# Up projection by channels: the weights as left operand, one pool of PSUM banks behind the mixer, the embedding ahead of it

## The chip, the core and the metric

The kernel runs on one core of a Trainium2 chip, as one program. A core has engines that each work through their own instructions in order and wait for each other by semaphores: TensorE (PE in the profile, with its weight loads as PEld), VectorE (DVE), ScalarE (ACT), GpSimd (POOL) and SyncE (SP, which here only issues transfers). TensorE multiplies a left operand, which is loaded ahead as weights (128 contraction rows x 128 columns here), with a right operand that streams through (128 contraction rows x up to 512 columns), and adds the product to a bank of PSUM; a bank holds 128 partitions x 512 float32, and there are eight. The metric is the device time of one execution in microseconds (us). Three executions of the kernel before took 1487.59, 1486.27 and 1486.39 us; the median is 1486.39.

## The reference

One layer of a hybrid decoder over 256 tokens (T) with a model width of 2048 (D), all in float32. Its first part, the mixer (state space heads and windowed attention, then an output projection that is added to h), is the same in both kernels. The rest is this:

```python
u = _rmsnorm(h, ffn_norm_g[i]) @ w_up[i]                  # 2048 -> 2 x 5632 channels
u = _causal_dwconv(u, ffn_conv_w[i], ffn_conv_b[i])       # 3 taps along the tokens, channel by channel
g_ff, u_ff = jnp.split(u, [D_FF], axis=-1)
h = h + (jax.nn.silu(g_ff) * u_ff) @ w_down[i]            # 5632 -> 2048
gate = jax.nn.sigmoid(_rmsnorm(h, ple_norm_g[i]) @ w_ple_gate[i])
pe = _rmsnorm(p[i] @ w_ple_proj[i], ple_post_g[i])        # the embedding: 256 -> 2048
h = h + gate * pe
```

`_rmsnorm` divides a token's row by the root of its mean square and multiplies each channel with a gain. The convolution shifts along the tokens, with weights of its own for each channel.

## The kernel before, in words

**Numbers and products.** Every operand of a matmul is split into a high part (a cast to a shorter type, `S.copy` on ScalarE, L195) and a low part (the rest, a subtraction on VectorE, L196). A product takes three matmuls into the same bank: high times high weights (L231), high times low weights (L232), low times high weights (L233). The left operand is a tile of activations, 128 channels x 128 tokens; the right operand is 128 channels x 512 columns of the weights; so a result has the tokens on its partitions, one bank for each of the two blocks of 128 tokens (`acc_pair`).

**Weights.** `load_w` (L201) loads 512 KB, a tile of 128 x 1024, from SyncE's queue into one of five buffers, ScalarE casts it (L195) and VectorE subtracts (L196), into four buffers each. One such tile serves two contraction steps of 128 of one chunk of 512 columns.

**Left operands.** Activations with tokens on the partitions have to be transposed to become a left operand: `transpose_split` (L257) lets TensorE transpose 128 x 128 pieces (L264) into a bank, and ScalarE and VectorE split the result (with a gain for each channel, L198 and L199) into the high and low tiles of an `Lhs` (L240 and on).

**Stages.** The mixer ends with output projections; the last one (L750) runs after the last attention heads, in four slices of 512 columns. After each slice `add_to_h` (L365) adds it to h, and `next_lhs` (L370) squares the new part of h (L374, for the norm) and transposes it unscaled, with the gains, into `hT`. The norm's factor `rh`, one number for each token, follows from all four slices (`finish_rstd`, L377). Two loads stand on ScalarE's queue here: the convolution's weights `fcw` (L759) and the transposed p (L766), which goes into the space of `pe` and is split into `ph` and `pl`. These tiles lie in space that the mixer's pools held until then.

The up stage (`up`, L784) runs over 22 chunks of 512 channels, eleven for the gate and eleven for u. A chunk takes eight weight tiles and 16 contraction steps of six matmuls, 96 in all. ScalarE moves its two banks out and multiplies with `rh` (L790), since the tokens lie on the partitions there. Then `conv_chunk` (L284) transposes the result, eight times 128 x 128 (L291), into two banks of the pool `ps_tr`, so that the channels lie on the partitions, and `conv_tile` (L275) makes the first tap with the bias on ScalarE (L278) and two more on VectorE (L280). Silu, the product with u (GpSimd) and a split make it the left operand of the down projection, which runs in six segments of up to two pairs of chunks, each one segment late. The last segment's projection squares and transposes h again for the gate. Then `embed` (L769) runs: four slices of two contraction steps, 48 matmuls, copied out to `pe` by VectorE (L778) and squared by ScalarE (L780). Last comes the gate stage: the post gain is loaded (on SyncE's queue), `pe` is normed, and for each of four slices 96 matmuls (L223) are followed by sigmoid, multiplication, addition and the store.

**What sets the order.** The code is recorded first, and a scheduler places it by a model of the engines: each engine's order is fixed when the program is built. Each pool's buffers set how far the work ahead may run: PSUM's eight banks belong to `ps_acc` (two tags, two buffers each), `ps_tr` (two) and `ps_ms` (two, used by the mixer).

## Time and profile before

| | before |
|---|---|
| median of three runs | 1486.39 us |
| the profiled execution | 1487.57 us |
| its span, from first to last instruction | 1485.8 us |
| mean granted TensorE clock | 1.000 |
| 0 to 637.4: mixer and output projections | 637.4 us, PE busy 632.11 |
| 637.4 to 1380.9: up and down projections | 743.5 us, PE busy 743.50 |
| 1380.9 to 1392.7: embedding | 11.8 us, PE busy 11.80 |
| 1392.7 to 1485.8: gate | 93.1 us, PE busy 88.08 |

The stages are stretches that were cut at the first and last matmul of each stage, read from the timeline; busy times are those of the view by windows. "Busy" of TensorE counts the modelled ends of pipelined matmuls, so busy is not the same as at its peak. A row of the timeline gives start and duration of an instruction in us, the engine, the line, the operation, result and operands; x6 at its end means six of them drawn together. A row of a group gives the count, the summed busy time in us, the mean of one in ns, and the idle time of the engine ahead of them. A row of windows gives from:to and length, the busy time of PE, PEld, DVE, ACT and POOL with their counts, then the granted clock, the share of the DMA engines and GB/s. In the strip by slices a 9 means nine tenths or more.

### The profile page before, as it was taken

The page shows a single profiled execution, that of the slowest core. Times are in us where ns is not written, and L with a number is a line of the kernel's source. Part 1 is how long each engine was busy: PE and PEld are TensorE (multiplying, and loading weights), DVE is VectorE, ACT ScalarE, POOL GpSimd, SP SyncE. Part 2 cuts the span into 40 slices and gives each one's busy share as a digit, 9 for nine tenths or more (in the row PEclk, how much of TensorE's full clock was granted, in tenths as well). Part 3 has the DMA queues.
Part 4 walks back from the last instruction along what each step waited for, and adds up shares of the span by engine and source line. Part 5 has one row for each costly group of instructions (what it writes and reads, how often), then busy time and mean ns, then how long its engine had stood idle before and what let it go on. Part 6 is the DMA issues. An engine that isn't in the chain of part 4 may idle for free.

```text
span 1485.8 us, 18615 instructions
## 1 busy us (share of the span) xinstructions
PE 1475.5 (99%) x6884; PEld 1213.0 (82%) x6884; DVE 977.0 (66%) x1290; ACT 800.3 (54%) x1111; POOL 159.2 (11%) x152
## 2 busy tenths in 40 slices
PE   9999999999999999999999999999999999999998
PEld 6887888888787888888888888888888888888887
DVE  7568776656769687766556656565665556566854
ACT  7575555646555454565555445545553554454643
POOL 1004022044033030000000000000000000000000
PEclk9999999999999999999999999999999999999999
DMA  9565665655555545366666666666566666656672
GB/s 338 180 205 170 202 184 167 185 158 179 145 164 148 157 148 163 115 196 199 185 186 187 191 188 184 185 196 187 184 191 191 184 188 192 185 186 189 206 226 100
DMA packets 79099, 271.67 MB, mean 183 GB/s; under 512 B 8752, under 2 KB 11504, under 8 KB 78624
## 3 DMA queue, kind: packets, MB, share of 16 engines
q1 hardware_dynamic: 78176, 269.55, 59.2%
q8 instruction: 54, 0.88, 0.2%
q10 hardware_dynamic: 720, 0.74, 0.1%
q0 software_dynamic: 112, 0.19, 0.1%
q14 instruction: 37, 0.30, 0.1%
HBM read 268.32 MB, written 2.13 MB: 182 GB/s over the span
## 4 chain that ended last, share of the span: by engine, by line
PE 95%; DMA 2%; DVE 1%; POOL 1%; issue 1%; ACT 0%; SPq 0%; DVEq 0%; POOLq 0%
PE acc L233 27%; PE acc L232 27%; PE acc L231 27%; PE acc L223 5%; PE tr L291 2%; PE ms L656 1%; PE acc L329 1%; PE ms L505 1%; PE acc L330 1%; PE acc L331 1%; DMA seg<-scr 1%; PE tr L264 1%; PE tr L688 1%; DMA w<-in_w_in_dram 1%; PE ms L698 0%
## 5 line engine op out<-in xcount | busy, mean ns | idle before, releaser
L196 DVE TENSOR_TENSOR wl<-w,wh 128x1024 fp32r<-128x1024 f32 (+1 forms) x493 | 617.8, 1256 | 396.5 <-ACT wh L195 395.1
L195 ACT CAST wh<-w 128x1024 fp32r<-128x1024 f32 (+1 forms) x493 | 516.5, 1050 | 485.7 <-PE acc L233 380.2
L232 PE MATMUL acc<-wl,ah 128*128 128x512 f32 x1168 | 457.0, 391 | 1.2 <-DVE wl L196 1.1
L233 PE MATMUL acc<-wh,al 128*128 128x512 f32 x1168 | 457.5, 394 | 0.0
L231 PE MATMUL acc<-wh,ah 128*128 128x512 f32 x1168 | 457.3, 393 | 0.0
L232 PEld LDWEIGHTS acc<-wl,ah 128*128 128x128 f32 x1168 | 219.4, 188 | 47.0 <-DVE wl L196 2.1
L231 PEld LDWEIGHTS acc<-wh,ah 128*128 128x128 f32 x1168 | 219.5, 188 | 45.7 <-issue 1.8
L233 PEld LDWEIGHTS acc<-wh,al 128*128 128x128 f32 x1168 | 219.0, 188 | 44.5 <-issue 0.8
L233 PE MATMUL acc<-wh,gl 128*128 128x512 f32 x352 | 137.6, 391 | 0.0
L231 PE MATMUL acc<-wh,gh 128*128 128x512 f32 x352 | 137.4, 390 | 0.0
L232 PE MATMUL acc<-wl,gh 128*128 128x512 f32 x352 | 137.2, 390 | 0.0
L806 POOL TENSOR_TENSOR cv<-cv,cv 128x1024 f32<-128x1024 f32 x11 | 35.5, 3228 | 649.2 <-DVE cv L280 649.2
L231 PE MATMUL acc<-wh,yh 128*128 128x512 f32 x256 | 100.2, 395 | 0.0
L232 PE MATMUL acc<-wl,yh 128*128 128x512 f32 x256 | 100.1, 392 | 0.0
L233 PE MATMUL acc<-wh,yl 128*128 128x512 f32 x256 | 99.8, 394 | 0.0
L280 DVE SCALAR_TENSOR_TENSOR cv<-tr,fcw,cv 128x254 f32<-128x254 f32 (+1 forms) x176 | 74.0, 476 | 19.8 <-ACT cv L278 19.8
L368 DVE TENSOR_TENSOR h<-h,acc 128x512 f32<-128x512 f32 x112 | 73.8, 680 | 6.0 <-PE acc L233 5.7
L232 PEld LDWEIGHTS acc<-wl,gh 128*128 128x128 f32 x352 | 66.1, 188 | 13.6
L233 PEld LDWEIGHTS acc<-wh,gl 128*128 128x128 f32 x352 | 66.1, 188 | 13.5
L231 PEld LDWEIGHTS acc<-wh,gh 128*128 128x128 f32 x352 | 66.1, 188 | 13.4
L278 ACT ACTIVATE cv<-tr,fcw 128x256 f32<-128x256 f32 x88 | 44.8, 559 | 34.3 <-PE tr L291 34.3
L233 PEld LDWEIGHTS acc<-wh,yl 128*128 128x128 f32 x256 | 48.1, 188 | 10.6 <-issue 1.0
(248 smaller groups left out, 1362.6 us busy)
## 6 DMA issues: line engine op xcount, KB each, us to landing
w<-in_w_up_dram SPq DMA_DIRECT2D x176, 512.0 KB, 3.7
w<-in_w_in_dram SPq DMA_DIRECT2D x127, 512.0 KB, 3.8
w<-in_w_down_dram SPq DMA_DIRECT2D x88, 512.0 KB, 3.7
w<-in_w_out_dram SPq DMA_DIRECT2D x64, 512.0 KB, 3.6
w<-in_w_pg_dram SPq DMA_DIRECT2D x32, 512.0 KB, 4.2
seg<-scr SPq DMA_DIRECT2D x8, 512.0 KB, 6.0
h<-in_x_dram SPq DMA_DIRECT2D x2, 1024.0 KB, 8.4
w<-in_w_pe_dram SPq DMA_DIRECT2D x4, 512.0 KB, 4.3
```

Of the source, the lines that this page charges most:

```text
L195: S.copy(hi, src)
L196: V.tensor_tensor(out=lo, in0=src, in1=hi.bitcast(F32), op=ALU.subtract)
L223: PE.matmul(acc[b], lhsT=l, rhs=r, start=(k == 0 and m == 0), stop=(k == total - 1 and m == 2))
L231: PE.matmul(acc[b], lhsT=hi, rhs=wh[:, i, :], start=(k == 0), stop=False)
L232: PE.matmul(acc[b], lhsT=hi, rhs=wl[:, i, :], start=False, stop=False)
L233: PE.matmul(acc[b], lhsT=lo, rhs=wh[:, i, :], start=False, stop=(k == total - 1))
L264: PE.transpose(tr[:, i, b * P : (b + 1) * P], src[b][:, f * P : (f + 1) * P], ident)
L278: S.activation(out=dst, in_=ps, func=AF.Identity, scale=taps[n - 1], bias=bias)
L280: V.scalar_tensor_tensor(out=dst[:, s:], in0=ps[:, : T - s], scalar=taps[n - 1 - s], in1=dst[:, s:], op0=ALU.mult, op1=ALU.add)
L291: PE.transpose(tr[:, i, b * P : (b + 1) * P], src[b][:, f * P : (f + 1) * P], ident)
L368: V.tensor_tensor(out=hs, in0=hs, in1=acc[b], op=ALU.add)
L806: G.tensor_tensor(out=cg, in0=cg, in1=cu, op=ALU.mult)
```

## The change

In `up`, the weights become the left operand, 128 input channels x 128 output channels, and the activations the right one. A chunk has four banks, one for each 128 channels, with the high and the low part of the activations side by side as 512 columns (2 x 256 tokens). For each contraction step and channel tile there are two matmuls: high weights times both halves (512 columns, L824 of the changed kernel) and low weights times the high half (256 columns, added to the second half of the bank, L825). So a chunk has 128 matmuls. ScalarE copies the first half of a bank out, VectorE adds the second, and the sum has the channels on its partitions already: it goes straight to `conv_tile`, with no transposes.

Since tokens now lie along the free axis there, `rh` can't be applied behind the product: h is multiplied with `rh` before it is transposed (L808, on VectorE). So the last output projection only squares its slices, and the 32 transposes of h follow when `rh` is known. `embed` is called ahead of them in place of behind the last down projection. The pools of PSUM of the mixer are closed there, and one pool `ps_b` of four tags with two buffers serves the embedding, the transposes, the up, down and gate stages. `Lhs` keeps high and low in one tile, so that both can be streamed as one operand.

```diff
@@ -92,9 +92,11 @@
     act = ctx.enter_context(tc.tile_pool(name="act", bufs=1))
     const = ctx.enter_context(tc.tile_pool(name="const", bufs=1))
     small = ctx.enter_context(tc.tile_pool(name="small", bufs=2))
-    ps_acc = ctx.enter_context(tc.tile_pool(name="ps_acc", bufs=2, space=PSUM))
-    ps_tr = ctx.enter_context(tc.tile_pool(name="ps_tr", bufs=2, space=PSUM))
-    ps_ms = ctx.enter_context(tc.tile_pool(name="ps_ms", bufs=2, space=PSUM))
+    banks = ExitStack()
+    ps_acc = banks.enter_context(tc.tile_pool(name="ps_acc", bufs=2, space=PSUM))
+    ps_tr = banks.enter_context(tc.tile_pool(name="ps_tr", bufs=2, space=PSUM))
+    ps_ms = banks.enter_context(tc.tile_pool(name="ps_ms", bufs=2, space=PSUM))
+    ps_b = []

     uid = [0]

@@ -117,10 +119,22 @@
         if n:
             G.memset(sb(pool, [P, n // 4], "fill", bufs=1), 0.0)

+    def bank(i):
+        return ps_b[0].tile([P, NC], F32, tag=f"b{i}", name=nm(f"bank{i}"))
+    took = [0, 0]
     def acc_pair():
+        if ps_b:
+            took[0] ^= 2
+            return [bank(took[0] + b) for b in range(NB)]
         return [ps_acc.tile([P, NC], F32, tag=f"acc{b}", name=nm(f"acc{b}")) for b in range(NB)]

     def tr_tile():
+        if ps_b:
+            took[1] = (took[1] + 1) % 4
+            return bank(took[1])
         return ps_tr.tile([P, NC], F32, tag="tr", name=nm("tr"))

     def ms_tile():
@@ -241,14 +255,15 @@


         def __init__(self, pool, kt, tag):
-            self.t = [
-                (sb(pool, [P, KG, T], f"{tag}h{g}", F32R), sb(pool, [P, KG, T], f"{tag}l{g}", F32R))
-                for g in range((kt + KG - 1) // KG)
-            ]
+            self.both = [sb(pool, [P, KG, 2, T], f"{tag}{g}", F32R) for g in range((kt + KG - 1) // KG)]
+            self.t = [(t[:, :, 0, :], t[:, :, 1, :]) for t in self.both]

         def part(self, k):
             h, l = self.t[k // KG]
             return h[:, k % KG, :], l[:, k % KG, :]
+        def pair(self, k):
+            return self.both[k // KG][:, k % KG, :, :]

         def __call__(self, k, b):
             h, l = self.part(k)
@@ -367,11 +382,14 @@
             hs = hres[b][:, n * NC : (n + 1) * NC]
             V.tensor_tensor(out=hs, in0=hs, in1=acc[b], op=ALU.add)

-    def next_lhs(lhs, ss, n, gain):
-
+    def squares(ss, n):
         for b in range(NB):
             sq = sb(small, [P, NC], "hsq")
             S.activation(out=sq, in_=hres[b][:, n * NC : (n + 1) * NC], func=AF.Square, accum_out=ss[:, b, n : n + 1])
+    def next_lhs(lhs, ss, n, gain):
+        squares(ss, n)
         transpose_split([hres[b][:, n * NC : (n + 1) * NC] for b in range(NB)], lhs, 4 * n, gain)

     def finish_rstd(ss, tag):
@@ -603,7 +621,6 @@
                 project(*held.pop(0))


-    hT = Lhs(act, KT, "a")
     ssh = sb(small, [P, NB, 4], "ssh", bufs=1)
     with tc.tile_pool(name="att_s", bufs=2) as as_, tc.tile_pool(name="att", bufs=2, reuse_waits="tile") as ap_:
         qscaled = sb(as_, [P, HD], "qgs", bufs=1)
@@ -747,10 +764,12 @@
                 project(*held.pop(0))
             prev_ = done
         fill(as_)
-        project(*prev_, lambda n: next_lhs(hT, ssh, n, g_ffn))
+        project(*prev_, lambda n: squares(ssh, n))

     rh = finish_rstd(ssh, "rh")
     mix.close()
+    banks.close()
+    ps_b.append(ctx.enter_context(tc.tile_pool(name="ps_b", bufs=2, space=PSUM)))


     pp = ctx.enter_context(tc.tile_pool(name="pe", bufs=1))
@@ -781,16 +800,36 @@

     with tc.tile_pool(name="ffn", bufs=2) as fp:

+        embed()
+        hT = Lhs(act, KT, "a")
+        for n in range(4):
+            hs = [sb(fp, [P, NC], f"hs{b}") for b in range(NB)]
+            for b in range(NB):
+                V.tensor_scalar_mul(hs[b], hres[b][:, n * NC : (n + 1) * NC], rh[:, b : b + 1])
+            transpose_split(hs, hT, 4 * n, g_ffn)
         def up(c):
-            acc = acc_pair()
-            gemm(acc, hT, [w_up[c, g] for g in range(KT // KW)])
-            t = []
-            for b in range(NB):
-                u_ = sb(fp, [P, NC], f"u{b}")
-                S.activation(out=u_, in_=acc[b], func=AF.Copy, scale=rh[:, b : b + 1])
-                t.append(u_)
+            acc = [bank(f) for f in range(4)]
+            for s in range(KT // KW):
+                wh, wl = load_w(w_up[c, s])
+                for i in range(KW):
+                    k = s * KW + i
+                    hl = hT.pair(k)
+                    for f in range(4):
+                        fs = slice(f * P, (f + 1) * P)
+                        PE.matmul(acc[f], lhsT=wh[:, i, fs], rhs=hl, start=(k == 0), stop=False)
+                        PE.matmul(acc[f][:, T:], lhsT=wl[:, i, fs], rhs=hl[:, 0, :], start=False, stop=(k == KT - 1))
             cv = sb(fp, [P, 4, T], f"cv{c // NPAIR}")
-            conv_chunk(t, cv, fcw, 3, 4 * c)
+            for f in range(4):
+                w = fcw[:, (4 * c + f) * 4 : (4 * c + f + 1) * 4]
+                u_ = sb(fp, [P, T], f"u{f}")
+                S.copy(u_, acc[f][:, :T])
+                V.tensor_tensor(out=u_, in0=u_, in1=acc[f][:, T:], op=ALU.add)
+                conv_tile(u_, cv[:, f, :], [w[:, j : j + 1] for j in range(3)], w[:, 3:4])
             return cv

         pair = 0
@@ -811,7 +850,6 @@
             pair += np_
         h2T = Lhs(act, KT, "a")
         project(*pending.pop(), lambda n: next_lhs(h2T, ssg, n, g_ple))
-        embed()
     rg = finish_rstd(ssg, "rg")
```

TensorE at the border between two chunks of the up stage, before: `acc` are the banks of the next chunk, `tr` those of the transposes, `u` the chunk that has just been moved out, `ah` and `al` the high and low part of the transposed h, `wh` and `wl` those of the weights.

```order
L231 MATMUL acc_1430_6921<-wh_6941,ah_507_2628 128x512
L232 MATMUL acc_1430_6921<-wl_6942,ah_507_2628 128x512
L291 MATMUL tr_6895<-ident_114,u_1424_6890 128x128
L291 MATMUL tr_6906<-ident_114,u_1424_6890 128x128
L233 MATMUL acc_1430_6921<-wh_6941,al_508_2629 128x512
L231 MATMUL acc_1429_6920<-wh_6941,ah_507_2628 128x512
L232 MATMUL acc_1429_6920<-wl_6942,ah_507_2628 128x512
L233 MATMUL acc_1429_6920<-wh_6941,al_508_2629 128x512
L291 MATMUL tr_6895<-ident_114,u_1425_6892 128x128
L291 MATMUL tr_6895<-ident_114,u_1424_6890 128x128
```

The same border in the changed kernel: `bank` is a bank of the new pool, `a` the tile with both parts of the transposed h.

```order
L824 MATMUL bank_1259_5976<-a_1237_5882,wh_6133 128x512
L825 MATMUL bank_1259_5976<-a_1237_5882,wl_6134 128x256
L824 MATMUL bank_1260_5977<-a_1237_5882,wh_6133 128x512
L825 MATMUL bank_1260_5977<-a_1237_5882,wl_6134 128x256
L824 MATMUL bank_1290_6180<-a_1234_5879,wh_6185 128x512
L825 MATMUL bank_1290_6180<-a_1234_5879,wl_6186 128x256
L824 MATMUL bank_1291_6181<-a_1234_5879,wh_6185 128x512
L825 MATMUL bank_1291_6181<-a_1234_5879,wl_6186 128x256
```

The transposes are gone, and long and short matmuls alternate, each with another tile of weights.

TensorE between the last output projection and the up stage, before: the projection's last slice has transposes of h (`h_1`, `h_2`, the two token blocks) among its matmuls, and the next rows are those of the first up chunk.

```order
L231 MATMUL acc_1240_5867<-wh_5869,ah_507_2628 128x512
L232 MATMUL acc_1240_5867<-wl_5870,ah_507_2628 128x512
L264 MATMUL tr_5692<-ident_114,h_1_84 128x128
L264 MATMUL tr_5692<-ident_114,h_2_85 128x128
L264 MATMUL tr_5692<-ident_114,h_1_84 128x128
L264 MATMUL tr_5692<-ident_114,h_2_85 128x128
L233 MATMUL acc_1239_5866<-wh_5869,al_508_2629 128x512
L233 MATMUL acc_1240_5867<-wh_5869,al_508_2629 128x512
L231 MATMUL acc_1239_5866<-wh_5887,ah_507_2628 128x512
```

The changed kernel there: the projection's last matmuls (`y` is its left operand) and the first of the embedding (`ph` is the high part of p).

```order
L245 MATMUL acc_1187_5699<-wh_5719,y_1044_5049 128x512
L246 MATMUL acc_1187_5699<-wl_5720,y_1044_5049 128x512
L247 MATMUL acc_1187_5699<-wh_5719,y_1044_5049 128x512
L245 MATMUL bank_1206_5775<-wh_5778,ph_5766 128x512
L246 MATMUL bank_1206_5775<-wl_5779,ph_5766 128x512
L245 MATMUL bank_1207_5776<-wh_5778,ph_5766 128x512
```

Of the 48 embedding matmuls 16 that need only `ph` come first, four for each slice; then each slice's other eight; then the 32 transposes of the scaled h (`hs`), and behind the last of these the up stage:

```order
L279 MATMUL bank_1252_5953<-ident_114,hs_1251_5950 128x128
L279 MATMUL bank_1253_5962<-ident_114,hs_1251_5950 128x128
L279 MATMUL bank_1253_5962<-ident_114,hs_1250_5949 128x128
L279 MATMUL bank_1253_5962<-ident_114,hs_1251_5950 128x128
L824 MATMUL bank_1259_5976<-a_1234_5879,wh_5979 128x512
L825 MATMUL bank_1259_5976<-a_1234_5879,wl_5980 128x256
L824 MATMUL bank_1260_5977<-a_1234_5879,wh_5979 128x512
```

Up matmuls, which stood among the transposes of h, now stand behind all of them.

VectorE in this place of the changed kernel: the copies of the embedding's banks into `pe` (L797), low halves of weights (L210), the scaling of the third and fourth slice of h (L808) and the first low halves of the transposed h (L213).

```order
L797 COPY pe_1199_5760<-bank_1227_5853 128x512
L210 TENSOR_TENSOR wl_6024<-w_6022,wh_6023 128x1024
L797 COPY pe_1200_5761<-bank_1228_5854 128x512
L808 TENSOR_SCALAR hs_1246_5927<-h_1_84,rh_5748 128x512
L808 TENSOR_SCALAR hs_1250_5949<-h_1_84,rh_5748 128x512
L808 TENSOR_SCALAR hs_1247_5928<-h_2_85,rh_5748 128x512
L210 TENSOR_TENSOR wl_6046<-w_6044,wh_6045 128x1024
L808 TENSOR_SCALAR hs_1251_5950<-h_2_85,rh_5748 128x512
L213 SCALAR_TENSOR_TENSOR a_1234_5879<-bank_1241_5896,gains_92,a_1234_5879 128x256
```

The first four scalings stand ahead of the first copy of the embedding, these four behind the last, since `hs` has two buffers a block.

ScalarE's queue at the border, in the changed kernel: the squares of h (L388), the two loads, casts of weights (L209), the cast of p (`ph`) and the squares of the embedding (L799).

```order
L388 ACTIVATE hsq_5738,ssh_2620<-h_1_84 128x512 [waits DVE_49,Activation_49]
L778 DMA fcw_5762<-in_ffn_cw_dram 128x352 [waits PE_49]
L785 DMA pe_1199_5760<-in_pT_dram 128x512
L209 CAST wh_5856<-w_5855 128x1024 [waits DMAHW1_49]
L388 ACTIVATE hsq_5740,ssh_2620<-h_2_85 128x512 [waits DVE_49,Activation_49]
L209 CAST ph_5766<-pe_1199_5760 128x512 [waits DMAHW6_49]
L799 ACTIVATE hsq_5796,ssp_5768<-pe_1199_5760 128x512 [waits DVE_49,Activation_49]
L209 CAST wh_5979<-w_5978 128x1024 [waits DMAHW2_49,PE_49]
```

Before, the load of `fcw` stood one square earlier and that of p at the same place; high halves of h and casts of up weights stood where the squares of the embedding stand now.

## The prediction

> **What bounds the kernel.** I read the page first: span, engine shares, granted clock, chain of waits. Times are microseconds; this profiled execution took 1487.57, of which 1485.8 are its span, and the median of the runs shown is 1486.39. I work out a difference against this execution and add it to the median, since both are the same kernel 0.1% apart.
>
> ```profile
> span 1485.8 us, 18615 instructions
> PE 1475.5 (99%) x6884; PEld 1213.0 (82%) x6884; DVE 977.0 (66%) x1290; ACT 800.3 (54%) x1111; POOL 159.2 (11%) x152
> PEclk9999999999999999999999999999999999999999
> PE 95%; DMA 2%; DVE 1%; POOL 1%; issue 1%; ACT 0%; SPq 0%; DVEq 0%; POOLq 0%
> ```
>
> TensorE has hardly a gap and carries 95% of the chain. So every matmul slot saved is time saved and every TensorE gap added is time lost, one for one; work on VectorE (66%) or ScalarE (54%) counts only where TensorE comes to wait for it. Durations of matmuls overlap, so I never add them up: I take the distance from one start to the next, from the timeline.
>
> **Removed: the transposes of the up result.** Here is one chunk boundary of the up stage.
>
> ```profile
> L291 PE MATMUL tr<-ident,u 128*128 128x128 f32 x176 | 26.3, 272 | 0.0
> 904.74 0.39 PE L233 MATMUL acc<-wh,al 128*128 128x512 f32 x1
> ...
> 913.36 0.40 PE L232 MATMUL acc<-wl,ah 128*128 128x512 f32 x1
> ...
> 914.74 0.82 PE L291 MATMUL tr<-ident,u 128*128 128x128 f32 x6
> ...
> 921.11 0.39 PE L232 MATMUL acc<-wl,ah 128*128 128x512 f32 x1
> ```
>
> From 904.74 to 913.36 stand 38 steps of 512-wide matmuls: 8.62 / 38 = 0.2268 each. From 913.36 to 921.11 stand 30 such steps and the eight transposes of one chunk (two before the six that are shown): 7.75 - 30 x 0.2268 = 0.95 for eight, 0.119 each with the disturbance behind them. Twenty-two chunks (176 in the group's row) make **-20.9**, all on the bound engine. The 32 transposes of h ahead of the up stage stay; they only move.
>
> **Added: short matmuls.** Per contraction step a chunk had six 512-wide matmuls; now it has, for each of four channel tiles, one 512-wide (high weights times high and low activations side by side) and one 256-wide (low weights times high). The columns are the same, 4 x 768 = 6 x 512, but there are 22 x 16 x 4 = 1408 pairs of a long and a short one in place of 1.5 long ones, 0.3402 each. A steady alternation of the two widths occurs nowhere in this trace; the nearest is in the attention, where they are mixed.
>
> ```profile
> 408.54 0.28 PE L696 MATMUL ms<-ph,vh 128*128 128x256 f32 x1
> 408.66 0.28 PE L697 MATMUL ms<-ph,vl 128*128 128x256 f32 x1
> 408.77 0.40 PE L231 MATMUL acc<-wh,ah 128*128 128x512 f32 x1
> 409.01 0.40 PE L232 MATMUL acc<-wl,ah 128*128 128x512 f32 x1
> 409.24 0.28 PE L698 MATMUL ms<-pl,vh 128*128 128x256 f32 x1
> ...
> 409.59 0.28 PE L698 MATMUL ms<-pl,vh 128*128 128x256 f32 x1
> 409.71 0.40 PE L233 MATMUL acc<-wh,al 128*128 128x512 f32 x1
> 409.94 0.39 PE L231 MATMUL acc<-wh,ah 128*128 128x512 f32 x1
> ...
> 527.05 0.40 PE L232 MATMUL acc<-wl,ah 128*128 128x512 f32 x1
> 527.29 0.40 PE L233 MATMUL acc<-wh,al 128*128 128x512 f32 x1
> ```
>
> The six short ones (408.54 to 408.77 and 409.24 to 409.71) take 0.70, 0.117 each; the three long ones behind them (408.77 to 409.24, 409.71 to 409.94) take 0.70, 0.234 each, not 0.2268. So a short matmul also makes the long ones after it slower for a while. A pair costs 0.351 by these rows, 0.0108 more than 1.5 long ones: **+15.2** over 1408 pairs. From both sides: at half a long one's price (0.1134) and no after-effect, the pair costs nothing extra, 0; with the slowest long one behind a short one (527.05 to 527.29, 0.24) and a short one of 0.12 (408.54 to 408.66), 0.36, it is +28. A pair of 0.2268 + 0.12 stands between, +9.3. I take 15.2, the mixed rows being nearest to what will run.
>
> The Trainium skill, "TensorE: Matmul & The Clock Gate", section "Back-to-back issue gap", gives N / 2.4 + 2.5 ns for a matmul of N columns: a pair would then cost 1.3 ns more than 1.5 long ones, an estimate of 1.8 in place of 15.2, and the whole sum would be -6.7. The trace does not follow it: the steady 512-wide step is 226.8 ns here, not 215.8.
>
> **Moved: the embedding and the transposes of h, to the border between output projection and up stage.** Before, h was transposed unscaled between projection matmuls, and the embedding ran near the end. Now nothing of the up stage can start until the norm of all of h is known, and the embedding is to fill that hole. Its left operand comes from p, which is loaded into pe, in space that the last projection still holds.
>
> ```profile
> 636.96 0.39 PE L233 MATMUL acc<-wh,yl 128*128 128x512 f32 x1
> 637.38 0.33 ACTq L759 DMA_DIRECT2D fcw<-in_ffn_cw_dram  x1
> 637.86 0.34 ACTq L766 DMA_DIRECT2D pe<-in_pT_dram  x1
> 641.67 0.62 ACT L195 CAST ph<-pe 128x512 fp32r<-128x512 f32 x1
> ...
> 1385.09 1.22 DVE L196 TENSOR_TENSOR wl<-w,wh 128x1024 fp32r<-128x1024 f32 x1
> 1386.22 0.68 DVE L778 COPY pe<-acc 128x512 f32<-128x512 f32 x1
> ...
> 1386.89 0.87 DVE L199 SCALAR_TENSOR_TENSOR al<-tr,gains,ah 128x256 fp32r<-128x256 f32 x2
> ...
> L532 DVE TENSOR_SCALAR yc<-yc,ry 128x512 f32<-128x512 f32 x8 | 3.5, 480 | 1.4 <-POOL ry L190 1.4
> ```
>
> I count from the start of the last projection matmul (636.96 = 0). Both loads leave ScalarE's queue only when that matmul has ended (0.42); the load of p lands and the cast starts at 4.7 and ends at 5.3. Before, up matmuls covered this; now the first embedding matmul, due at 0.23, starts at 5.3. The 48 embedding matmuls (four slices, two contraction steps, two token blocks, three products) end at 5.3 + 48 x 0.2268 = 16.2; half of the transposes of h follow at once. The other half needs the third and fourth slice of scaled h, and these stand in VectorE's queue behind all eight copies of the embedding (0.61 each) and three weight halves (1.13 each). The first copy can start at 9.9 (in TensorE's order 16 matmuls with the high half of p, for all slices, come first, and four more finish the first bank: 20), so 8.3 of such work ends at 18.2, and about 18.9 with the casts that ScalarE owes it in between. Then four scalings (0.48, overlapping to 0.4) and one more weight half: 21.7. Only then do the low halves of the transposed h start, 0.4 each; the first up matmul needs seven of them for its operand and for its bank: 24.6, and two further banks hold back its neighbours to 25.8, with 0.7 of matmuls done in between. So the up stage runs from 25.1 as if without a gap. Of these 24.9 since 0.23, the embedding (10.9) and 32 transposes (3.8) were paid before as well: **+10.2**. Bounds: 8 if p lands sooner and the casts fall in better, 12.5 if they fall worse.
>
> Behind the two waiting loads ScalarE's queue holds the cast of the last embedding weights and the last square of h, both done before p lands; behind the cast of p stand the squares of the copies, four weight casts and the high halves of h, in this order, and TensorE waits for those. On SyncE's queue the four embedding weight loads now stand ahead of the up weights instead of ahead of the gate weights; the up matmuls start 25 later, so this costs nothing.
>
> The up stage itself is covered: per chunk of 22 VectorE has eight weight halves, four additions and eight taps, ScalarE eight casts, four copies and four first taps.
>
> ```profile
> L196 DVE TENSOR_TENSOR yl<-ms,yh 128x256 fp32r<-128x256 f32 x16 | 6.7, 419 | 7.2 <-ACT yh L195 7.2
> L195 ACT CAST yh<-ms 128x256 fp32r<-128x256 f32 x16 | 6.0, 373 | 26.1 <-PE ms L698 26.0
> L278 ACT ACTIVATE cv<-tr,fcw 128x256 f32<-128x256 f32 x88 | 44.8, 559 | 34.3 <-PE tr L291 34.3
> ppg<-in_ppg_dram SPq DMA_DIRECT2D x1, 1024.0 KB, 7.1
> ```
>
> With 0.42 for an addition, 0.37 for a copy and 0.56 for a first tap or (taken alike) any later tap that is 15 and 12 of 22: cost 0, hidden behind the next chunk's matmuls, and four weight buffers stand ahead. At the end the embedding no longer covers the last transposes and the load of the post gain (7.1 to landing). The low halves of the last slice then stand behind two long VectorE multiplications, about 17 after the last down matmul; the gate matmuls that need them come some 17.5 to 19 after it. Cost 0, up to 2 if that cover fails.
>
> **The clock.** Two gaps of 5.1 and about 7 (the second broken by transposes) may cost more than their length.
>
> ```profile
> 6.00 2.05 PE L329 MATMUL acc<-wh,ah 128*128 128x512 f32 x4 [0.59 <-DVE ah L317]
> 8.70 1.05 PE L331 MATMUL acc<-wh,al 128*128 128x512 f32 x2
> 9.55 0.63 PE L330 MATMUL acc<-wl,ah 128*128 128x512 f32 x1
> 10.40 0.39 PE L330 MATMUL acc<-wl,ah 128*128 128x512 f32 x1
> 10.62 0.40 PE L331 MATMUL acc<-wh,al 128*128 128x512 f32 x1
> 1480.39 0.39 PE L233 MATMUL acc<-wh,al 128*128 128x512 f32 x1
> 1481.00:1484.90 3.90, 0.00 (x0) 0.00 (x0) 1.79 (x6) 0.66 (x2) 0.00 (x0) 1.00 0.38 134
> 1484.95:1485.80 0.85, 0.00 (x0) 0.00 (x0) 0.00 (x0) 0.00 (x0) 0.00 (x0) 0.50 0.00 0
> ```
>
> At the start a matmul takes (9.55 - 8.70) / 2 = 0.43, and 0.22 from 10.40 on: 4.4 of work at half speed since 6.00 loses 2.2. At the end the granted clock falls to 0.50 some 4.5 after the last matmul began. So one such gap is just long enough. I take one drop, **+2.2**; bounds 0 and 4.4.
>
> The Trainium skill, "TensorE: Matmul & The Clock Gate", Part 1, says that one idle window of about 3.4, on a free-running grid, halves the clock, and a busy one restores it; the window rows agree with that size. Its Part 4 says that transposes do not count as busy: by that the second gap drops the clock too and the sum rises by 2.2, which no run here shows.
>
> **The sum.** -20.9 + 15.2 + 10.2 + 2.2 = +6.7, slower: 1493.1. A measurement of this kernel tells a change from none at about 0.2%, 3.0.
>
> **Rivals.** *Short matmuls at their columns' price*, faster: alternating widths settle at 0.340 to 0.3468 a pair. For it: a short one of 0.11 (408.66 to 408.77), half a long one, and the long one at 409.94 starts a steady run again. Against it: the long ones of 0.234 that follow short ones. It gives 6.7 - 15.2 + (0 to 9.3), that is -8.5 to +0.8, about 1482.5; it decides as soon as the pair stays below 0.3462, where the sum is 0, and is faster by over 3.0 below 0.3441. The Trainium skill's section on the back-to-back issue gap, quoted above, speaks for this one. *A cheaper border*: p lands early and the clock holds: 6.7 - 2.2 - 2.2 = +2.3, 1488.7. For it: weight loads pause there, so the queue is short; against it: 3.8 from the issue of p's load (637.86) to its cast (641.67). *A dearer one*: pairs of 0.36 and two clock drops, 6.7 + 12.7 + 2.2 = +21.6, 1508. For it: the 0.24 behind a short one; against it: that is the slowest of several. That the transposes were not on the path is excluded by the first rows; the order of the changed kernel has none in the up stage.
>
> **How the numbers follow.** Forecast 0.50, first rival 0.30, cheaper border 0.10, dearer one 0.10. Faster by over 0.2%: 0.17 of the first rival and 0.03 of the second, 0.20. Within: 0.13 of the first, 0.05 of the second, 0.03 of the forecast, 0.21. Slower: 0.47 of the forecast, 0.02 of the cheaper border, 0.10 of the dearer one, 0.59. The forecast's own range, from the bounds of border and clock and pairs of 0.3485 to 0.354, is 1486 to 1502. The whole range reaches down to 1480, past most of the first rival, and up to 1504, which leaves most of the dearer one out.
>
> **What will show it.** In the changed profile: the distance from one long matmul's start to the next in the up stage, 0.351 or 0.340; a gap near 5 on TensorE ending with the cast of p, a second one ending with the low halves of h; the granted clock in the slices behind both; no TensorE wait at later chunk borders. Wrong it would be above all if the pair comes out near 0.340, or if the up stage waits for VectorE at every chunk.

## The result, and the profile after

| | before | after |
|---|---|---|
| median of five runs | 1486.47 us | 1499.15 us |
| the profiled execution | 1487.57 us | 1501.33 us |
| its span | 1485.8 us | 1499.6 us |
| mean granted TensorE clock | 1.000 | 0.995 |

The ratio is 1.0087, its 95% interval 1.0077 to 1.0098: slower by 12.7, where 6.7 were forecast. These are the lines of the changed kernel's page that answer to those of before: span, busy times, clock strip, and the two groups of the new matmuls.

```profile
span 1499.6 us, 19813 instructions
PE 1479.2 (99%) x7412; PEld 1233.9 (82%) x7412; DVE 1017.7 (68%) x1386; ACT 799.0 (53%) x1155; POOL 151.9 (10%) x152
PEclk9999999999999999989999999999999999999999
L824 PE MATMUL bank<-a,wh 128*128 128x512 f32 x1408 | 499.4, 400 | 1.2 <-DVE a L213 1.2
L825 PE MATMUL bank<-a,wl 128*128 128x256 f32 x1408 | 396.1, 281 | 0.0
```

TensorE is still "99% busy", so the page alone doesn't say where 13.8 of span came from. The one 8 in the clock strip and the idle time of 1.2 behind a low half (`a`, L213) point to the border. The timeline there, engines mixed:

```profile
635.85 0.39 PE L247 MATMUL acc<-wh,y 128*128 128x512 f32 x1
636.64 0.46 ACTq L785 DMA_DIRECT2D pe<-in_pT_dram  x1
639.79 0.71 POOL L204 TENSOR_TENSOR rh<-rs_t,nhalf 128x2 f32<-128x2 f32 x1 [3.36 <-DVE rs_t L202]
642.66 0.62 ACT L209 CAST ph<-pe 128x512 fp32r<-128x512 f32 x1 [3.86 <-DMA pe<-in_pT_dram]
643.32 0.69 DVE L210 TENSOR_TENSOR pl<-pe,ph 128x512 fp32r<-128x512 f32 x1 [3.60 <-ACT ph L209]
643.34 0.79 PE L245 MATMUL bank<-wh,ph 128*128 128x512 f32 x1 [7.09 <-ACT ph L209]
...
659.26 1.27 DVE L808 TENSOR_SCALAR hs<-h,rh 128x512 f32<-128x512 f32 x3
661.98 6.35 DVE L213 SCALAR_TENSOR_TENSOR a<-bank,gains,a 128x256 fp32r<-128x256 f32 x16
664.85 0.79 PE L824 MATMUL bank<-a,wh 128*128 128x512 f32 x1 [1.20 <-DVE a L213]
```

The first embedding matmul waits for the cast of p, which waits 6.0 for its load; the second half of the scalings comes at 659.26, the low halves at 661.98, the up stage at 664.85. The clock beside it, by windows (the column ahead of the last two):

```profile
635.85:643.34 7.49, 0.40 (x3) 0.01 (x1) 3.20 (x6) 3.01 (x6) 0.83 (x2) 0.86 0.86 321
643.34:648.13 4.79, 4.79 (x11) 3.79 (x12) 2.25 (x5) 0.00 (x0) 0.00 (x0) 0.51 0.00 1
...
658.29:661.70 3.41, 1.81 (x12) 1.04 (x10) 3.41 (x7) 3.41 (x12) 0.00 (x0) 1.00 0.68 221
...
664.85:668.72 3.87, 3.87 (x13) 3.33 (x14) 3.48 (x9) 1.64 (x4) 0.00 (x0) 0.52 0.04 15
```

Two drops, one behind each gap: 11 matmuls take 4.79 where 11 x 0.2268 = 2.49 were due (2.3 lost), and six pairs take 3.87 (1.75 lost by the pair below). The row of 658.29 to 661.70 is the stretch just ahead of the second drop: TensorE was busy with transposes for 1.81 of its 3.41. The price of a pair is read over one chunk, from the start of its first long matmul to that of the next chunk's first; the last row is the kernel's last matmul:

```profile
711.83 0.40 PE L824 MATMUL bank<-a,wh 128*128 128x512 f32 x1
...
734.44 0.40 PE L824 MATMUL bank<-a,wh 128*128 128x512 f32 x1
...
1494.14 0.39 PE L247 MATMUL bank<-wh,a 128*128 128x512 f32 x1
```

(734.44 - 711.83) / 64 = 0.3533 a pair, 0.0131 over 1.5 long ones: 18.4 for 1408 pairs. (All chunks but the first, which holds the clock loss, have 0.3531 to 0.3535.) From the last projection matmul to the last matmul of all it is 843.43 before (1480.39 - 636.96) and 858.29 after, 14.9 more. The parts: -20.9 for the transposes of u, +18.4 for the pairs, and the border. That is 664.85 - 635.85 - 0.23 = 28.8, with the second clock loss 30.5, against 10.9 for the embedding and 2.9 for the 24 transposes of h that stood behind that matmul before: +16.8. The sum is 14.3; 0.6 is left over.

### The profile page after: what moved, and what is told of

Read it like the earlier page. It is cut to its first block, busy times and chain, and to the rows that moved or that the text cites. A ratio compares the mean times of both kernels' runs of the same rounds, so it can differ in the third digit from the quotient of the medians.

```text
span 1499.6 us, 19813 instructions
## 1 busy us (share of the span) xinstructions
PE 1479.2 (99%) x7412; PEld 1233.9 (82%) x7412; DVE 1017.7 (68%) x1386; ACT 799.0 (53%) x1155; POOL 151.9 (10%) x152
## 4 chain that ended last, share of the span: by engine, by line
PE 94%; DVE 2%; DMA 2%; issue 1%; POOL 1%; ACT 0%; SPq 0%; ACTq 0%; DVEq 0%; POOLq 0%
PE bank L824 22%; PE bank L825 11%; PE acc L247 10%; PE acc L245 10%; PE acc L246 10%; PE bank L245 6%; PE bank L246 6%; PE bank L247 6%; PE bank L237 5%; PE ms L673 1%; PE acc L344 1%; PE acc L345 1%; PE acc L346 1%; PE ms L523 1%; DMA seg<-scr 1%; PE tr L705 1%
## 5 line engine op out<-in xcount | busy, mean ns | idle before, releaser
L210 DVE TENSOR_TENSOR wl<-w,wh 128x1024 fp32r<-128x1024 f32 (+1 forms) x493 | 624.1, 1268 | 383.5 <-ACT wh L209 381.8
L209 ACT CAST wh<-w 128x1024 fp32r<-128x1024 f32 (+1 forms) x493 | 516.3, 1049 | 547.0 <-PE bank L824 195.2
L824 PE MATMUL bank<-a,wh 128*128 128x512 f32 x1408 | 499.4, 400 | 1.2 <-DVE a L213 1.2
L825 PE MATMUL bank<-a,wl 128*128 128x256 f32 x1408 | 396.1, 281 | 0.0
L824 PEld LDWEIGHTS bank<-a,wh 128*128 128x128 f32 x1408 | 265.4, 188 | 67.8 <-DVE a L213 1.6
L825 PEld LDWEIGHTS bank<-a,wl 128*128 128x128 f32 x1408 | 266.8, 190 | 0.2
L246 PE MATMUL acc<-wl,a 128*128 128x512 f32 x448 | 176.6, 394 | 1.1 <-DVE wl L210 1.0
L247 PE MATMUL acc<-wh,a 128*128 128x512 f32 x448 | 176.9, 395 | 0.0
L245 PE MATMUL acc<-wh,a 128*128 128x512 f32 x448 | 176.4, 395 | 0.0
L245 PE MATMUL bank<-wh,g 128*128 128x512 f32 x352 | 137.3, 390 | 0.0
L246 PE MATMUL bank<-wl,g 128*128 128x512 f32 x352 | 137.3, 390 | 0.0
L247 PE MATMUL bank<-wh,g 128*128 128x512 f32 x352 | 137.0, 389 | 0.0
L245 PE MATMUL acc<-wh,y 128*128 128x512 f32 x256 | 100.2, 394 | 0.0
L247 PE MATMUL acc<-wh,y 128*128 128x512 f32 x256 | 99.8, 394 | 0.0
L245 PEld LDWEIGHTS acc<-wh,a 128*128 128x128 f32 x448 | 84.2, 188 | 18.5 <-issue 1.8
L247 PEld LDWEIGHTS acc<-wh,a 128*128 128x128 f32 x448 | 84.2, 188 | 17.5 <-issue 0.8
L245 PEld LDWEIGHTS bank<-wh,g 128*128 128x128 f32 x352 | 66.1, 188 | 13.8
```

The lines of the kernel that those rows point to most:

```text
L209: S.copy(hi, src)
L210: V.tensor_tensor(out=lo, in0=src, in1=hi.bitcast(F32), op=ALU.subtract)
L245: PE.matmul(acc[b], lhsT=hi, rhs=wh[:, i, :], start=(k == 0), stop=False)
L246: PE.matmul(acc[b], lhsT=hi, rhs=wl[:, i, :], start=False, stop=False)
L247: PE.matmul(acc[b], lhsT=lo, rhs=wh[:, i, :], start=False, stop=(k == total - 1))
L824: PE.matmul(acc[f], lhsT=wh[:, i, fs], rhs=hl, start=(k == 0), stop=False)
```

## The experiments

Each run is given with its median and its ratio to the kernel before on the same chip.

**g4 and g8: is it the short matmul or the switch of width?** The up loop of the changed kernel in another order; g4, and in g8 the same over both contraction steps of a weight tile (eight and eight):

```diff
                     for f in range(4):
                         fs = slice(f * P, (f + 1) * P)
                         PE.matmul(acc[f], lhsT=wh[:, i, fs], rhs=hl, ...)
+                    for f in range(4):
+                        fs = slice(f * P, (f + 1) * P)
                         PE.matmul(acc[f][:, T:], lhsT=wl[:, i, fs], rhs=hl[:, 0, :], ...)
```

> Only the order of the up matmuls changes: for each contraction step the four long ones first, then the four short ones. In the changed kernel a pair of a long and a short one takes 0.354 (0.2373 + 0.1173), against 0.3402 for 1.5 steady long ones. Theory A (price of the short one): a short matmul takes 0.118 wherever it stands and the long ones behind it 0.232 to 0.236; then the pair becomes 0.350 to 0.354 and the time 1494 to 1499. Theory B (price of the switch of width): what is lost is lost where the width changes; with a quarter of the switches the pair becomes 0.3437 and the time 1499.2 - 14.5 = 1484.7.

> As the run before, with eight long ones and then eight short ones for each weight tile. Theory A: the pair 0.349 to 0.353, time 1492 to 1498. Theory B: the pair 0.3419, time 1499.2 - 17 = 1482. The two runs together tell whether the loss goes with the number of short ones or with the number of switches.

g4 took 1497.28 (1.0076, 1.0060 to 1.0093), g8 1495.73 (1.0064, 1.0049 to 1.0079). The timeline of TensorE at the starts of two chunks that follow each other, g4 first and then g8:

```profile
710.75 0.86 PE L824 MATMUL bank<-a,wh 128*128 128x512 f32 x3
...
733.20 0.87 PE L824 MATMUL bank<-a,wh 128*128 128x512 f32 x3
```

```profile
711.63 0.86 PE L824 MATMUL bank<-a,wh 128*128 128x512 f32 x3
...
733.97 0.86 PE L824 MATMUL bank<-a,wh 128*128 128x512 f32 x3
```

22.45 / 64 = 0.3508 and 22.34 / 64 = 0.3491. With an eighth of the switches 0.0042 of the 0.0131 goes and 0.0089 stays, so most of the loss goes with the number of short ones: theory A.

**early_p: the load of p.** The load and the split stand ahead of the last projection, in tiles of the left operand that is no longer used there:

```diff
+        pt_ = sb(act, [P, KG, 2, T], "a2")[:, 0, :, :]
+        php = sb(act, [P, KG, 2, T], "a3", F32R)
+        ph, pl = php[:, 0, :, :], php[:, 1, :, :]
+        nc.scalar.dma_start(pt_, pT)
+        split(pt_, ph, pl)
         project(*prev_, lambda n: squares(ssh, n))
...
-    nc.scalar.dma_start(pt_, pT)
-    split(pt_, ph, pl)
```

> The transposed p is loaded and split before the last output projection, into space that the old left operand left free, so the embedding has its operand when the projection ends. In the changed kernel TensorE stands idle for 7.1 there and then runs eleven matmuls at half clock (2.2 lost). If this wait is the cause, both go: the first embedding matmul follows within 1 of the last projection matmul, the first up matmul comes 8 to 10 earlier and the time is 1489 to 1492. Rival: VectorE's chain (norm, copies, scalings, low halves) sets the start of the up stage anyway; then the second gap grows by what the first loses, and the time falls by 4 at most, to 1495 or more.

1490.31 (1.0024, 1.0013 to 1.0035), 8.8 below the changed kernel: the place of this load was the cause of so much of the loss. TensorE there:

```profile
637.10 0.39 PE L247 MATMUL acc<-wh,y 128*128 128x512 f32 x1
638.96 0.47 PE L245 MATMUL bank<-wh,a 128*128 128x512 f32 x1 [1.47 <-ACT wh L209]
...
649.97 2.78 PE L279 MATMUL bank<-ident,hs 128*128 128x128 f32 x24
653.33 1.27 PE L279 MATMUL bank<-ident,hs 128*128 128x128 f32 x8 [0.58 <-DVE hs L807]
656.47 0.66 PE L823 MATMUL bank<-a,wh 128*128 128x512 f32 x1 [1.87 <-DVE a L213]
```

The embedding starts 1.9 after the projection's last matmul (behind the cast of its last weights), and the up stage 19.4 after it in place of 29.0.

**embed_last: what the embedding covers.** The changed kernel with the embedding back behind the last down projection:

```diff
-        embed()
         hT = Lhs(act, KT, "a")
...
         project(*pending.pop(), lambda n: next_lhs(h2T, ssg, n, g_ple))
+        embed()
```

> The changed kernel with nothing but the embedding back at the end. Theory: the embedding is no cover for the border, since its own operand comes as late as the norm; bare, the border is set by the norm (rh 640.5 in the changed kernel, 4.7 after the last projection matmul), the scalings and the chain of splits, so the up stage starts about 13 to 15 after that matmul, a clock drop of 2 behind it: 12 to 13 over the 3.8 of the transposes, against 15.8, time 1495 to 1497. Rival: without the embedding nothing hides the norm and the scalings at all and the time is above 1499.

1495.19 (1.0056, 1.0042 to 1.0070): at the lower edge of the expected time, and the reason holds only in part. The up stage starts 13.6 after the last projection matmul (637.88 to 651.49), as expected. The timeline ahead of it:

```profile
645.08 0.62 ACT L209 CAST ph<-pe 128x512 fp32r<-128x512 f32 x1 [4.24 <-DMA pe<-in_pT_dram]
645.73 0.69 DVE L210 TENSOR_TENSOR pl<-pe,ph 128x512 fp32r<-128x512 f32 x1 [3.98 <-ACT ph L209]
646.34 1.67 DVE L807 TENSOR_SCALAR hs<-h,rh 128x512 f32<-128x512 f32 x4
```

Even without the embedding the scalings come behind the low half of p, which stands ahead of them in VectorE's queue and waits for the load. So in the changed kernel the load of p holds up two engines: the embedding on TensorE, and the scalings, whose norm was ready at 640.5 but which began at 643.92.

The clock drop that was expected behind the border lies inside it. TensorE stood idle for 8.65, and the granted clock fell to 0.50 meanwhile. Then 24 transposes ran without a wait, the first 20 of them at half clock. Behind these the clock was at 1.00 again, ahead of the first up matmul (one row of the timeline, then the windows):

```profile
646.92 4.81 PE L279 MATMUL bank<-ident,hs 128*128 128x128 f32 x24 [8.65 <-issue]
646.92:651.04 4.12, 4.12 (x20) 4.03 (x21) 3.44 (x9) 2.39 (x6) 0.00 (x0) 0.50 0.00 0
651.04:651.49 0.45, 0.45 (x7) 0.45 (x5) 0.45 (x3) 0.18 (x1) 0.00 (x0) 1.00 0.00 0
```

**early_p_hs4: the scalings' place in VectorE's queue.** early_p with one edit:

```diff
-            hs = [sb(fp, [P, NC], f"hs{b}") for b in range(NB)]
+            hs = [sb(fp, [P, NC], f"hs{b}", bufs=4) for b in range(NB)]
```

> early_p with four buffers in place of two for each half of the scaled h, so that VectorE scales all four slices before most of the embedding's copies, in its order too. In early_p TensorE still stood idle for 4.9 at the border (1.86, 0.85 and 2.14) and lost about 1.4 to the clock behind it. Theory: the last two slices waited behind the copies for their buffers; then the transposes follow the embedding without the 0.85, the low halves start earlier, and the time falls by 2 to 4, to 1486.5 to 1488.5. Rival: VectorE's whole work up to the first low half (eight copies, four weight halves, eight scalings) is the same in any order, so the first up matmul comes at the same time as in early_p (19.4 after the last projection matmul) and the time stays within 1 of 1490.3.

1489.25 (1.0013, 1.0001 to 1.0024), 1.1 less, inside the spread of both (ten runs each, 1487.7 to 1492.3 and 1486.1 to 1493.6). TensorE's wait at the end of the border:

```profile
656.96 0.79 PE L823 MATMUL bank<-a,wh 128*128 128x512 f32 x1 [3.40 <-DVE a L213]
```

The last projection matmul began at 637.04 in this run, so the up stage starts 19.9 after it, against 19.4: the rival's start holds, and its time, within 1 of 1490.3, is missed by 0.1. VectorE's sum of work set the start in both orders.

**late_norm: the border taken away.** h is transposed unscaled inside the last projection as before, the norm comes after the sum, the embedding is last:

```diff
+    for b in range(NB):
+        V.tensor_scalar_mul(dg[:, b * P : (b + 1) * P], ident, rh[:, b : b + 1])
...
+        PE.matmul(tr[:, :T], lhsT=one, rhs=dg, start=True, stop=True)
+        S.copy(rb, tr[:, :T])
...
                 V.tensor_tensor(out=u_, in0=u_, in1=acc[f][:, T:], op=ALU.add)
+                G.tensor_tensor(out=u_, in0=u_, in1=rb, op=ALU.mult)
...
-        embed()
-        hT = Lhs(act, KT, "a")
-        for n in range(4):
-            hs = ...
+        project(*prev_, lambda n: next_lhs(hT, ssh, n, g_ffn))
```

> The up product stays by channels, but h is transposed unscaled inside the last output projection as before the change, the norm's factor is spread over the partitions once by a small matmul and multiplied in after the sum, by GpSimd, and the embedding stands at the end again. The whole border goes. If the border is worth the 15.8 that the two traces show (30.5 from the last projection matmul to an even start of the up stage, clock loss included, against 10.9 + 3.8 for the embedding and the transposes alone), the time is 1499.2 - 15.8 = 1483.4, and 1481 to 1487 with a short wait at the first chunk. Rival: GpSimd's 88 multiplications, about 0.6 each, hold up the chunks, and TensorE waits at each chunk; then the time stays above 1490.

1495.97 (1.0068, 1.0053 to 1.0083): a miss, and not by the rival named. TensorE at the border:

```profile
635.32 1.03 PE L279 MATMUL tr<-ident,h 128*128 128x128 f32 x8
640.23 1.09 PE L279 MATMUL tr<-ident,h 128*128 128x128 f32 x4 [3.88 <-DVE rs_t L202]
642.37 1.09 PE L279 MATMUL tr<-ident,h 128*128 128x128 f32 x4 [1.06 <-DVE a L213]
645.03 1.94 PE L279 MATMUL tr<-ident,h 128*128 128x128 f32 x8 [1.57 <-DVE a L213]
649.17 0.77 PE L828 MATMUL bank<-a,wh 128*128 128x512 f32 x1 [2.20 <-DVE a L213]
```

The transposes stand alone here, with two buffers to go through, and no up matmul is among them.

**late_norm_open: the pools stay open.** The only difference to late_norm is where the banks behind the mixer come from (in part):

```diff
-    banks.close()
-    ps_b.append(ctx.enter_context(tc.tile_pool(name="ps_b", bufs=2, space=PSUM)))
...
+        def four():
+            odd[0] ^= 1
+            return acc_pair() + acc_pair() if odd[0] else [ms_tile(), ms_tile(), tr_tile(), tr_tile()]
```

> As late_norm, but the mixer's PSUM pools stay open: a chunk of the up stage takes the four accumulator banks or the four others in turn, so that the last transposes of h can stand among the first up matmuls. In late_norm TensorE stood idle for 10.2 at the border (4.15, 1.48, 1.99 and 2.62) and then ran seven matmuls at half clock (about 2). Theory: the closed pools kept the up matmuls behind all transposes, and these waited for the two buffers of their own; then gaps and clock loss go and the time is 1496.0 - 12 = 1484. If the pair then falls into the faster of the two rhythms that late_norm showed (0.3467 in its chunks 1 to 7, 0.3533 in the later ones), it is up to 9 less. Rival: the wait for the left operand's low halves on VectorE comes in place of the one removed, and the time stays above 1490.

1481.93 (0.9966, 0.9954 to 0.9979), faster than before the change. The border, and the last matmul:

```profile
635.43 0.39 PE L247 MATMUL acc<-wh,y 128*128 128x512 f32 x1
635.66 0.62 PE L832 MATMUL acc<-a,wh 128*128 128x512 f32 x2
...
636.34 0.60 PE L279 MATMUL tr<-ident,h 128*128 128x128 f32 x4
...
1476.79 0.39 PE L247 MATMUL acc<-wh,a 128*128 128x512 f32 x1
```

Up matmuls start at the next step and the transposes stand among them. From 635.43 to 1476.79 it is 841.36, 2.1 less than before the change; -20.9 + 18.4 = -2.5. So these two terms alone, without a border, are nearly nothing. The medians differ by more, 5.8 (1487.71 before, on this chip). The profiled execution took 1483.99, the second slowest of the five (1480.21 to 1485.42), so a part of the gain was not traced.

**late_norm_open_g8: both together**, the order of g8 in this kernel.

> The run before with eight long and then eight short matmuls for each weight tile. The pair was 0.3492 in g8 against 0.3533: 0.0041 x 1408 = 5.8 less than the run before if that is in the slow rhythm, 1478; if it is in the fast one (0.3467), 3.5 more. Against the kernel before the change: -20.9 for the transposes + 1408 x 0.009 = 12.7, so 1486.4 - 8.2 = 1478.

1479.41 (0.9944, 0.9931 to 0.9958): the best of all, 0.56% below the kernel before the change.

**all_512: the control.** In late_norm_open the product of the low weights goes over the whole bank:

```diff
-                        PE.matmul(acc[f][:, T:], lhsT=wl[:, i, fs], rhs=hl[:, 0, :], ...)
+                        PE.matmul(acc[f], lhsT=wl[:, i, fs], rhs=hl, ...)
```

> late_norm_open with the product of the low weights 512 columns wide as well: it adds the product of the two low parts, which the kernel leaves out otherwise. Theory A (the price is that of the short matmuls): with the weights as left operand and long matmuls alone each step is 0.2268, as in the other stages, so 2816 of them take 1408 x (0.4536 - 0.3533) = 141 more than late_norm_open: 1623. Rival: the new form costs something by itself (the weights as left operand, four banks in turn), then the step is above 0.228 and the time above 1626.

One run, 1629.4. Two chunk starts and the bounds, from the timeline:

```profile
639.68 0.39 PE L247 MATMUL acc<-wh,y 128*128 128x512 f32 x1
...
730.29 0.39 PE L832 MATMUL ms<-a,wh 128*128 128x512 f32 x1
...
759.30 0.39 PE L832 MATMUL acc<-a,wh 128*128 128x512 f32 x1
...
1622.22 0.39 PE L247 MATMUL acc<-wh,a 128*128 128x512 f32 x1
```

29.01 / 128 = 0.2266 a step, and 982.54 from the last projection matmul to the end, 141.2 over late_norm_open: just the price of long ones. (The total is above 1626 since this run's earlier part was longer: the last projection matmul comes at 639.68, against 635.43.) Weights as left operand and four banks in turn cost nothing; the loss comes with the short matmuls.

**late_norm_open_sl: why some chunks ran faster.** In late_norm's chunks 1 to 7 (the first chunk is 0) a pair took less than later on. Two neighbouring chunk starts early in the stage, and two late in it:

```profile
696.20 0.39 PE L828 MATMUL bank<-a,wh 128*128 128x512 f32 x1
...
718.39 0.39 PE L828 MATMUL bank<-a,wh 128*128 128x512 f32 x1
...
895.47 0.40 PE L828 MATMUL bank<-a,wh 128*128 128x512 f32 x1
...
918.08 0.40 PE L828 MATMUL bank<-a,wh 128*128 128x512 f32 x1
```

22.19 / 64 = 0.3467 and 22.61 / 64 = 0.3533, with the same instructions in the same order. The experiment puts the short one ahead from the second contraction step on:

```diff
+                        if k:
+                            PE.matmul(acc[f][:, T:], lhsT=wl[:, i, fs], rhs=hl[:, 0, :], ...)
                         PE.matmul(acc[f], lhsT=wh[:, i, fs], rhs=hl, ...)
+                        if not k:
+                            PE.matmul(acc[f][:, T:], lhsT=wl[:, i, fs], rhs=hl[:, 0, :], ...)
-                        PE.matmul(acc[f][:, T:], lhsT=wl[:, i, fs], rhs=hl[:, 0, :], ...)
```

> As late_norm_open, with the short matmul ahead of the long one from the second contraction step on, so that two short ones follow each other once in each chunk. If the two rhythms are a matter of the phase at which the alternation starts, the pair becomes 0.3467 in some or all chunks, worth up to 9; if the rhythm belongs to the alternation as such and late_norm's first chunks had another cause, it is 0.3533 throughout and the time that of late_norm_open within 1.

1483.04 (0.9968, 0.9957 to 0.9979), no gain. Three chunk starts from its timeline:

```profile
685.30 0.40 PE L834 MATMUL acc<-a,wh 128*128 128x512 f32 x1
...
707.52 0.39 PE L834 MATMUL ms<-a,wh 128*128 128x512 f32 x1
...
730.13 0.39 PE L834 MATMUL acc<-a,wh 128*128 128x512 f32 x1
```

22.22 / 64 = 0.3472, then 22.61 / 64 = 0.3533. The fast rhythm appears in five of the 22 chunks, and four of these are the first behind a down projection. So the same alternation runs in either rhythm, and what stands ahead of a chunk seems to matter, but in late_norm the chunks behind a down projection were slow; what sets the rhythm stays open. The fast rhythm is also cheaper than the groups of eight in g8 (0.3491), which have an eighth of its switches: the number of switches alone does not set the price of a pair.

## Why the prediction was right in sign and range, and short in size

The four terms were the right ones, and their errors did not cancel: the pairs came out 3.2 higher, the border 1.6 and the clock 1.9, together 6.7, where the median is 6.0 above the forecast. (By the prediction's own bounds the lower end of its range is 1485 and not 1486: -20.9 + 11.7 + 8 + 0 = -1.2.)

- **Transposes of u, -20.9.** Together with the pairs they make -2.1 in late_norm_open and -7.7 in late_norm_open_g8 (1472.07 - 636.29 = 835.78 against 843.43), where the sums of the terms are -2.5 and -20.9 + 1408 x (0.3491 - 0.3402) = -8.4. That fits within 0.7. all_512 sets the term apart from the pairs: 982.54 - 843.43 = 139.1 more than before, of which 704 more long matmuls (2816 in place of 2112) at 0.2268 are 159.7, so -20.6 is left.

```profile
636.29 0.39 PE L247 MATMUL acc<-wh,y 128*128 128x512 f32 x1
...
1472.07 0.39 PE L247 MATMUL acc<-wh,a 128*128 128x512 f32 x1
```

- **Pairs, +15.2, measured +18.4.** The attention's mixed rows had the mechanism (a short one of 0.117, slower long ones behind it) and a pair of 0.351; in the steady alternation it is 0.3533, inside the bounds. The first rival, the columns' price, is excluded in this profile, where no chunk is below 0.3531; its upper end, 0.3468, is near the fast rhythm that some chunks of other runs showed (0.3467).
- **Border, +10.2.** In the measure used there (32 transposes paid before) it is 28.8 less the 2.3 of the first clock loss, 26.5 - 14.7 = +11.8, inside the bounds of 8 to 12.5. The step that was too small is the load of p: the embedding starts 7.3 after it was due, not 5.1. Its load took 6.0 in place of 3.8. Why is open: up weights were being loaded in both kernels, with the DMA engines 0.96 busy under this load and 0.94 before, and the same load took 4.4 in late_norm and 6.4 in embed_last. The weight loads did not pause there, as the cheaper border had it. The rest of that chain came out nearly as written: the first up matmul came at 29.0, and without these 2.2 and the 2.3 of the clock that is 24.5, against 24.6; the hold-up by two further banks, 0.5, did not come.
- **Clock, +2.2, measured 2.3 + 1.75 = 4.05.** One drop was taken and there were two, near the upper bound of 4.4. The rule named there, Part 4 of the Trainium skill's "TensorE: Matmul & The Clock Gate", by which transposes don't count as busy, gave this second drop, but the traces don't agree with the rule. In embed_last 4.12 of transposes without a wait, and no other matmul, brought the clock back from 0.50 to 1.00. In the changed kernel the transposes had waits among them and behind them (1.36, 0.66 and 1.20), and TensorE was busy for only 1.81 of the 3.41 ahead of the drop. So the waits are left as the cause; no run varied them alone.
- **The section "Back-to-back issue gap"** of the same page of the Trainium skill gives its formula for isolated matmuls; the estimate from it was 1.8 for the pairs, and 18.4 were measured. Another section of that Trainium skill page, "LDWEIGHTS (loading the stationary operand)", gives about P / 1.2 ns for P columns, an estimate of 107 ns for 128, hardly less than the 0.117 that a short matmul takes here. That could explain why a short one can't hide the next load; no run here varied the load, so it is argued, not shown.
- **Covers.** As forecast, no matmul of the later chunks waits for VectorE or ScalarE. The end costs nothing: the span ends 5.5 after the last matmul began (1499.6 - 1494.14), 5.4 before.

## What to carry to other kernels

A transposition saved is worth only what the new operand layout doesn't give back: here 256-wide matmuls cost 0.009 to 0.013 each over their columns in most chunks, which took 12 to 18 of 20.9. Take the price of a mixture from rows that have the mixture in its order, not from a steady run of either width, and look whether it has more than one rhythm; grouping by width took away a third of the loss against the slow one. And where a row factor forces a norm ahead of a product, look first for a place behind the product: with the factor multiplied in after the sum, by an engine that had time, and with pools that let the next stage start, the same idea won 0.56% where it had lost 0.87%.

## What the runs showed of the hardware that was not expected

- The same alternation of long and short matmuls has two steady rhythms, 0.3467 and 0.3533 a pair. In early_p_hs4 the fast one held for seven chunks, 7 x 64 x 0.0066 = 3.0, and in late_norm for six and a part of a seventh. early_p's spread of 7.5 over ten runs may come from it; that was not traced.
- Transposes alone can bring the full clock back (embed_last, 646.92 to 651.04), and they can hold it. In early_p nothing but transposes ran from 649.97 to 656.47; TensorE was busy for 2.93 of the 3.42 from 649.82 on and the clock stayed at 1.00. It fell to 0.50 at 656.65, behind a stretch with a wait of 1.87, in which TensorE was busy for only 1.45 of 3.41:

```profile
653.24:656.65 3.41, 1.45 (x9) 1.02 (x10) 3.41 (x10) 3.41 (x11) 0.00 (x0) 1.00 0.56 165
```

- GpSimd's multiplication of 128x256 took 1.04, not the 0.6 scaled from its 128x1024 ones (mean of the group of 88 in late_norm_open); the 88.8 in all lay beside matmuls.
